# Gates and branch products of two hybrid layers with the tokens on the partitions

## The chip, the cores and the metric

The kernel runs on one core of a Trainium2 chip. The metric is the device time of one execution in microseconds (us); lower is better. The core's engines are named as in the profile: PE is TensorE (matrix products), PEld its weight loads, DVE VectorE, ACT ScalarE, POOL GpSimd, SP SyncE, which issues most transfers.

## The reference

Two blocks stand one behind the other, on 256 tokens of 1024 features in float32: a first one (pool attention, feed-forward, recurrent layer, feed-forward) and two "hybrid" layers. The change touches the hybrid layers alone. One of them, cut to what matters:

```python
h = rms_norm_2(x, g_mix)
proj = h @ w_in
... s_q, s_k, s_v, gate_logits = jnp.split(proj, offs, axis=-1)
o_mla = mla_attention(q, k, v_mla).reshape(b, s, BRANCH_WIDTH)
o_diff = (rms_norm_2(od, g_diff_out) * (1.0 - lam_init)).reshape(b, s, BRANCH_WIDTH)
o_win = window_attention(wq, wk, wv, positions, win_sink, slopes[:WIN_HEADS])
gates = jax.nn.sigmoid(gate_logits.reshape(b, s, N_BRANCH, D_MODEL))
merged = (gates[:, :, 0] * (o_mla @ w_branch[0])
          + gates[:, :, 1] * (o_diff @ w_branch[1])
          + gates[:, :, 2] * (o_win @ w_branch[2]))
x = x + merged @ w_out
```

Three gates of 1024 columns each come from the normed input (1024 features), three branch products of 1024 columns from the three attentions (512 features each). Gate times branch, summed over the three, is `merged`, which goes through the output product.

## The kernel before

**Products.** Each operand is split in a rounded part (`hi`, `xh`) and the rest (`lo`, `xl`), and `mm3` issues three matmuls for each product: hi by hi, hi by lo, lo by hi. Weights come as a stream of chunks of 1 MB through the SP queue into `st`; ACT rounds a chunk to `hi` in two halves (L262), DVE subtracts to get `lo` in two halves (L263). `st`, `hi` and `lo` have three buffers each, so the next chunk's first half on ACT waits until PE has done with the chunk three back.

**Two layouts.** The query product of a hybrid layer has tokens as the stationary operand (a slice of 128 tokens of `xh`) and 512 weight columns as the moving one; its result has tokens on the partitions. Gates and branch products are the other way round: 128 weight columns stationary, all 256 tokens moving, features on the partitions. So a gate of 1024 columns is 8 column groups by 8 slices of features by 3 = 192 matmuls of 256 columns, and a branch product is 96.

**Norm factors.** The norm's factor of each token, `r`, is applied behind the products. With features on the partitions it has to lie along the columns: `norm_rows` spreads it by two small products with `ones` (L411) into `rb`, and `times_r` (L604, DVE) multiplies a gate's bank by it before ACT takes the tanh (L1241). A sigmoid is computed as half of tanh(z/2) + 1; the half is applied when `merged` is split.

**Order around the change.** `hybrid` (phase 5 is the first hybrid layer, phase 6 the second; they stand in the names as `_5_` and `_6_`) runs the norm and some projections, and then a list of "bursts": short attention pieces (scores, transposes of the weights of a softmax, their products), and between two of them one or more steps of "filler" work from `parts()`: query, gate 0, gate 1, branch 0, gate 2, branch 1. PE keeps this program order (`InOrder`, recorded at line L207). A step is 24 matmuls of 256 columns or 12 of 512. Behind the bursts stand `branch(2)` and the output product, in four parts `kk` = 0, 2, 4, 6 of one chunk and 24 matmuls of 512 each, in banks A, A, A and O. Here the scheduler decides.

**The merge.** A branch's bank is multiplied by (gate + 1) on DVE (L1256, L1258) and summed (L1259) into `merged`, 128 by 512 four times. In `branch(2)` each quarter is split at once: ACT writes half of it to `mh` (L1263, named `xh`), DVE the rest to `ml` (L1264, named `xl`). They lie as the output product needs them, with features on the partitions.

**PSUM.** The banks are A (3), S (2), T (2) and O (1). Transposes of the softmax weights go to T; ACT copies them from there to `pT` (L853), and the O products read `pT`.

**A small input.** Behind the output product's code stands the load of `pe` (POOL queue) and its split (L311 on ACT); the scheduler places both among the bursts, where the trace shows them as `w<-in_pe_dram` and `w<-w`.

Of the kernel before, what the change touches and what calls it, by code (L numbers as in the profile page):

```python
# [11 lines left out]
F32 = mybir.dt.float32  # L12
F32R = mybir.dt.float32r
# [6 lines left out]
P = 128  # L20
S = 256
# [43 lines left out]
def _stream(a):  # L65
# [11 lines left out]
    for i in range(2):  # L77
# [11 lines left out]
        for kind, b in MERGE:  # L89
            if kind == "gate":  # L90
                out += [_kt(w, 0, KD, o[9] + b * D + j * 256, o[9] + b * D + j * 256 + 256) for j in range(4)]
                continue
# [117 lines left out]
class Net:  # L210
# [204 lines left out]
    def r_times(self, c):  # L415
        z = self.t([P, 16], "ty")
        self.nc.vector.tensor_scalar(z[:, :2], self.r, c, None, op0=ALU.mult)
        return z
# [780 lines left out]
    def hybrid(self, i, g0):  # L1199
# [5 lines left out]
        self.norm_rows()  # L1205
# [12 lines left out]
        def query():  # L1218
            b = [self.bank("A"), self.bank("A")]
            for k0 in (0, 4):  # L1220
                wh, wl = self.chunk(4, 512)
                for t in range(2):
                    for k in range(4):
                        kk, c = k0 + k, slice(t * P, t * P + P)
                        self.mm3(b[t], xh[:, kk, c], xl[:, kk, c], wh[:, k, :], wl[:, k, :], kk == 0, kk == KD - 1)
                    yield
            self.copy_out(b, 512, wq)
            self.headnorm(wq, 8, 64)

        def gate(b):  # L1230
            for jp in range(4):
                bk = self.bank("A")
                wh, wl = self.chunk(KD, 256)
                for e in range(2):
                    for k in range(KD):
                        c = slice(e * P, e * P + P)
                        self.mm3(bk[:, e * S:e * S + S], wh[:, k, c], wl[:, k, c], xh[:, k, :], xl[:, k, :], k == 0, k == KD - 1)
                    if e == 0:
                        yield
                g = self.times_r(self.t([P, 2, S], "hg"), bk).rearrange("p e s -> p (e s)")  # L1240
                nc.scalar.activation(g, g, AF.Tanh, scale=0.5)  # L1241
                gates[b].append(g)
                yield

        def branch(b):
            if b == 2:
                mh, ml = self.halves = self.t([P, KD, S], "xh", F32R), self.t([P, KD, S], "xl", F32R)
            for jp in range(4):
                if jp % 2 == 0:
                    wh, wl = self.chunk(4, 512)  # L1250
                bk = self.bank("A")
                self.fm_pair(bk, *outs[b], wh, wl, 4, (jp % 2) * 256)
                m = merged[jp // 2][:, jp % 2, :]
                g = gates[b][jp]
                if b == 0:
# [109 lines left out]
```

## Time and profile before

| | us |
|---|---|
| median of 3 runs | 1517.9 (1517.53 to 1520.76) |
| profiled execution, its own time | 1523.45 |
| its span in the trace | 1521.7 |
| mean granted TensorE clock | 0.997 |

The profiled execution is the one that the rows below show. The granted clock has two levels, 2.4 GHz (1.00 in the rows) and 1.2 GHz (0.50); a stretch that holds both shows a number between.

### The profile page before, as it was taken

To read this page: it belongs to the slowest core of one execution; us is meant where nothing else is said; L and a number is where in the kernel's file an instruction comes from. 1 tells how busy PE (TensorE), PEld (TensorE's weight loads), DVE (VectorE), ACT (ScalarE), POOL (GpSimd) and SP (SyncE) were. 2 spreads that over 40 slices of the span, in tenths; PEclk is the share of its full clock that TensorE was granted. 3 is DMA by queue.
4 is the path that set the end of the run, shared out by engine and by line. 5 is a ranking of instruction groups with operands and counts; after the bars stand their busy time and mean duration, and the time that the engine had idled before them with its cause. 6 is when DMAs were issued, how large, how long until landed. Compare 5 with 4: busy or idle time off the path is not lost.

```text
span 1521.7 us, 25363 instructions
## 1 busy us (share of the span) xinstructions
PE 1501.2 (99%) x10020; PEld 1356.4 (89%) x10020; DVE 1141.3 (75%) x2197; ACT 913.6 (60%) x1615; POOL 119.8 (8%) x109
## 2 busy tenths in 40 slices
PE   8999999999999999999999999999999999999998
PEld 6789999898999998889988999988889988999986
DVE  6659777789897777966867866668885877866666
ACT  6756555686775556755665545556856664654454
POOL 0200000000000000022530000000023250000000
PEclk9999999999999999999999999999999999999999
DMA  8445554445464554533334555544453344455551
GB/s 290 166 170 193 191 191 174 165 139 183 151 219 169 194 183 151 208 119 115 137 131 166 182 181 191 182 178 159 170 194 112 123 148 167 166 194 173 188 194 56
DMA packets 37879, 257.34 MB, mean 169 GB/s; under 512 B 4384, under 2 KB 4768, under 8 KB 8320
## 3 DMA queue, kind: packets, MB, share of 16 engines
q1 hardware_dynamic: 36576, 252.38, 46.8%
q0 software_dynamic: 896, 3.28, 0.6%
q8 instruction: 78, 1.28, 0.3%
q14 instruction: 41, 0.34, 0.1%
q10 hardware_dynamic: 288, 0.07, 0.0%
HBM read 254.66 MB, written 1.05 MB: 168 GB/s over the span
## 4 chain that ended last, share of the span: by engine, by line
PE 92%; DVE 3%; ACT 2%; POOL 1%; issue 1%; DMA 1%; SPq 0%; DVEq 0%
PE A L207 11%; PE A L279 11%; PE A L280 11%; PE A L281 10%; PE S L281 6%; PE S L280 6%; PE S L279 6%; PE T L281 6%; PE T L280 6%; PE T L279 6%; PE O L279 2%; PE O L280 2%; PE O L281 2%; PE S L207 2%; PE T L207 2%; PE O L207 1%
## 5 line engine op out<-in xcount | busy, mean ns | idle before, releaser
L263 DVE TENSOR_TENSOR lo<-st,hi 128x1024 fp32r<-128x1024 f32 (+3 forms) x480 | 573.6, 1209 | 129.4 <-ACT hi L262 126.7
L262 ACT ACTIVATE hi<-st 128x1024 fp32r<-128x1024 f32 (+3 forms) x480 | 489.2, 1043 | 264.4 <-PE T L280 109.7
L281 PE MATMUL S<-xh,lo 128*128 128x256 f32 x752 | 213.9, 284 | 0.0
L280 PE MATMUL S<-xl,hi 128*128 128x256 f32 x752 | 213.0, 283 | 0.0
L279 PE MATMUL S<-xh,hi 128*128 128x256 f32 x752 | 211.7, 282 | 0.0
L281 PE MATMUL T<-xh,lo 128*128 128x256 f32 x704 | 200.3, 285 | 0.0
L280 PE MATMUL T<-xl,hi 128*128 128x256 f32 x704 | 199.7, 284 | 0.0
L279 PE MATMUL T<-xh,hi 128*128 128x256 f32 x704 | 198.8, 282 | 0.0
L279 PEld LDWEIGHTS S<-xh,hi 128*128 128x128 f32 x752 | 142.5, 190 | 0.1
L281 PEld LDWEIGHTS S<-xh,lo 128*128 128x128 f32 x752 | 142.0, 189 | 0.1
L280 PEld LDWEIGHTS S<-xl,hi 128*128 128x128 f32 x752 | 141.5, 188 | 0.0
L279 PEld LDWEIGHTS T<-xh,hi 128*128 128x128 f32 x704 | 133.4, 189 | 1.6
L280 PEld LDWEIGHTS T<-xl,hi 128*128 128x128 f32 x704 | 132.5, 188 | 1.5
L281 PEld LDWEIGHTS T<-xh,lo 128*128 128x128 f32 x704 | 133.0, 189 | 0.1
L1074 POOL TENSOR_SCALAR s<-s,at 128x256 f32<-128x256 f32 x64 | 68.4, 1085 | 647.8 <-DVE ty L324 347.8
L280 PE MATMUL A<-lo,hg 128*128 128x512 f32 x294 | 116.3, 396 | 0.5 <-DVE lo L263 0.5
L279 PE MATMUL A<-hi,xh 128*128 128x512 f32 (+2 forms) x304 | 116.4, 385 | 0.2 <-ACT xh L389 0.2
L280 PE MATMUL A<-lo,xh 128*128 128x512 f32 (+2 forms) x304 | 116.3, 382 | 0.0
L279 PE MATMUL A<-hi,hg 128*128 128x512 f32 x294 | 116.2, 395 | 0.0
L281 PE MATMUL A<-hi,hg 128*128 128x512 f32 x294 | 116.2, 395 | 0.0
L281 PE MATMUL A<-hi,xl 128*128 128x512 f32 (+2 forms) x304 | 115.7, 383 | 0.0
L207 PE MATMUL A<-xh,hi 128*128 128x256 f32 x384 | 113.7, 296 | 0.0
(366 smaller groups left out, 3120.4 us busy)
## 6 DMA issues: line engine op xcount, KB each, us to landing
st<-in_w_dram SPq DMA_DIRECT2D x230, 1024.0 KB, 4.8
st<-in_w_dram SPq DMA_DIRECT2D x4, 832.0 KB, 4.5
st<-in_w_dram SPq DMA_DIRECT2D x2, 768.0 KB, 4.3
x<-in_x_dram SPq DMA_DIRECT2D x2, 512.0 KB, 5.0
st<-in_w_dram SPq DMA_DIRECT2D x4, 256.0 KB, 6.4
st<-in_w_dram SPq DMA_DIRECT2D x2, 512.0 KB, 3.5
w<-in_gain_dram POOLq DMA_DIRECT2D x2, 512.0 KB, 4.6
out_dram<-x SPq DMA_DIRECT2D x4, 256.0 KB, 2.0
```

The lines of the kernel that those rows point to most:

```text
L207: return lambda *a, **k: self.tc.keep_in_program_order(f(*a, **k))
L262: nc.scalar.activation(hi[:, c0:c1], st[:, c0:c1], AF.Copy)
L263: nc.vector.tensor_tensor(out=lo[:, c0:c1], in0=st[:, c0:c1], in1=hi[:, c0:c1].bitcast(F32), op=ALU.subtract)
L279: mm(out, ah, bh, start=start, stop=False)
L280: mm(out, ah, bl, start=False, stop=False)
L281: mm(out, al, bh, start=False, stop=stop)
L1074: nc.gpsimd.tensor_scalar(s[:, c], s[:, c], r[:, t:t + 1], None, op0=ALU.mult)
```

## The change

Gates and branch products now have the query's form: `columns` takes 128 tokens as the stationary operand and 512 weight columns as the moving one. A gate is 96 matmuls of 512 columns in place of 192 of 256; a branch product is 48 in place of 96. A step is 12 matmuls in place of 24, and their number stays. The chunks keep their bytes; a gate's chunk holds half the features of 512 columns in place of all the features of 256.

With tokens on the partitions `r` is a factor of each partition, so ACT takes the tanh straight from the bank with a scale of `half_r` (L1243 of the new file), and `times_r` and `norm_rows` go from the hybrid layers. `merged` has tokens on the partitions and has to be transposed for the output product: `turned(n)` does half of it by eight PE transposes (L1265) into one S and one T bank, two ACT copies (L1268) and two DVE subtractions (L1269); it is called ahead of `kk` = 0 and of `kk` = 4. New lines stand one or more further down than old ones (L279 to L281 become L280 to L282).

```diff
@@ -88,7 +88,8 @@
         out += [_kt(sq, 0, 4, 0, 512), _kt(sq, 4, 8, 0, 512)]
         for kind, b in MERGE:
             if kind == "gate":
-                out += [_kt(w, 0, KD, o[9] + b * D + j * 256, o[9] + b * D + j * 256 + 256) for j in range(4)]
+                for c in (o[9] + b * D, o[9] + b * D + 512):
+                    out += [_kt(w, 0, 4, c, c + 512), _kt(w, 4, 8, c, c + 512)]
                 continue
             wb = a["w_branch_2"][i, b]
             if b == 2:
@@ -413,8 +414,8 @@
         nc.scalar.activation(self.rb, pb[:, :S], AF.Copy)
 
     def r_times(self, c):
-        z = self.t([P, 16], "ty")
-        self.nc.vector.tensor_scalar(z[:, :2], self.r, c, None, op0=ALU.mult)
+        z = self.t([P, 2], "rg")
+        self.nc.vector.tensor_scalar(z, self.r, c, None, op0=ALU.mult)
         return z
 
 
@@ -1202,7 +1203,7 @@
         if i:
             self.layer_scalars(i)
         c, kr, skr = self.mla_prep(i, xh, xl)
-        self.norm_rows()
+        half_r = self.r_times(0.5)
         dq = self.proj(xh, xl, 8)
         dk = self.proj(xh, xl, 8)
         ch, cl = self.mla_low_rank(i, c)
@@ -1215,54 +1216,57 @@
         bursts, outs = self.heads(i, (q4, k4, v), (dq, dk, dv), (wq, wk, wv))
 
 
-        def query():
+        def columns(xh, xl, nk):
+
             b = [self.bank("A"), self.bank("A")]
-            for k0 in (0, 4):
+            for k0 in range(0, nk, 4):
                 wh, wl = self.chunk(4, 512)
                 for t in range(2):
                     for k in range(4):
                         kk, c = k0 + k, slice(t * P, t * P + P)
-                        self.mm3(b[t], xh[:, kk, c], xl[:, kk, c], wh[:, k, :], wl[:, k, :], kk == 0, kk == KD - 1)
+                        self.mm3(b[t], xh[:, kk, c], xl[:, kk, c], wh[:, k, :], wl[:, k, :], kk == 0, kk == nk - 1)
+                    yield t, (b[t] if k0 + 4 == nk else None)
+
+        def query():
+            for t, b in columns(xh, xl, KD):
+                if b is not None:
+                    nc.scalar.activation(wq[:, t, :], b, AF.Copy, scale=self.r[:, t:t + 1])
+                    if t == 1:
+                        self.headnorm(wq, 8, 64)
+                yield
+
+        def gate(b):
+            for n in range(2):
+                for t, bk in columns(xh, xl, KD):
+                    if bk is not None:
+                        g = self.t([P, 512], "hg")
+                        nc.scalar.activation(g, bk, AF.Tanh, scale=half_r[:, t:t + 1])
+                        gates[b].append(g)
                     yield
-            self.copy_out(b, 512, wq)
-            self.headnorm(wq, 8, 64)
-
-        def gate(b):
-            for jp in range(4):
-                bk = self.bank("A")
-                wh, wl = self.chunk(KD, 256)
+
+        def branch(b):
+            for n in range(2):
+                for t, bk in columns(*outs[b], 4):
+                    m, g = merged[n][:, t, :], gates[b][2 * n + t]
+                    if b == 0:
+                        nc.vector.scalar_tensor_tensor(m, g, 1.0, bk, op0=ALU.add, op1=ALU.mult)
+                    else:
+                        nc.vector.scalar_tensor_tensor(g, g, 1.0, bk, op0=ALU.add, op1=ALU.mult)
+                        nc.vector.tensor_tensor(out=m, in0=m, in1=g, op=ALU.add)
+                    yield
+
+        def turned(n, mh, ml):
+
+            for kp in range(2):
+                pt = self.bank("ST"[kp])
                 for e in range(2):
-                    for k in range(KD):
-                        c = slice(e * P, e * P + P)
-                        self.mm3(bk[:, e * S:e * S + S], wh[:, k, c], wl[:, k, c], xh[:, k, :], xl[:, k, :], k == 0, k == KD - 1)
-                    if e == 0:
-                        yield
-                g = self.times_r(self.t([P, 2, S], "hg"), bk).rearrange("p e s -> p (e s)")
-                nc.scalar.activation(g, g, AF.Tanh, scale=0.5)
-                gates[b].append(g)
-                yield
-
-        def branch(b):
-            if b == 2:
-                mh, ml = self.halves = self.t([P, KD, S], "xh", F32R), self.t([P, KD, S], "xl", F32R)
-            for jp in range(4):
-                if jp % 2 == 0:
-                    wh, wl = self.chunk(4, 512)
-                bk = self.bank("A")
-                self.fm_pair(bk, *outs[b], wh, wl, 4, (jp % 2) * 256)
-                m = merged[jp // 2][:, jp % 2, :]
-                g = gates[b][jp]
-                if b == 0:
-                    nc.vector.scalar_tensor_tensor(m, g, 1.0, bk, op0=ALU.add, op1=ALU.mult)
-                else:
-                    nc.vector.scalar_tensor_tensor(g, g, 1.0, bk, op0=ALU.add, op1=ALU.mult)
-                    nc.vector.tensor_tensor(out=m, in0=m, in1=g, op=ALU.add)
-                if b == 2:
-                    d = (slice(None), slice(2 * jp, 2 * jp + 2), slice(None))
-                    m2 = m.rearrange("p (e s) -> p e s", e=2)
-                    nc.scalar.activation(mh[d], m2, AF.Copy, scale=0.5)
-                    nc.vector.scalar_tensor_tensor(ml[d], m2, 0.5, mh[d].bitcast(F32), op0=ALU.mult, op1=ALU.subtract)
-                yield
+                    for t in range(2):
+                        c = (2 * kp + e) * P
+                        self.pe.transpose(pt[:, e * S + t * P:e * S + t * P + P], merged[n][:, t, c:c + P], self.ident)
+                d = (slice(None), slice(4 * n + 2 * kp, 4 * n + 2 * kp + 2), slice(None))
+                z = pt.rearrange("p (e s) -> p e s", e=2)
+                nc.scalar.activation(mh[d], z, AF.Copy, scale=0.5)
+                nc.vector.scalar_tensor_tensor(ml[d], z, 0.5, mh[d].bitcast(F32), op0=ALU.mult, op1=ALU.subtract)
 
         def parts():
             yield from query()
@@ -1281,9 +1285,11 @@
         self.pe = nc.tensor
         for _ in branch(2):
             pass
-        mh, ml = self.halves
+        mh, ml = self.t([P, KD, S], "xh", F32R), self.t([P, KD, S], "xl", F32R)
         acc = self.wide_banks()
         for kk in range(0, 8, 2):
+            if kk % 4 == 0:
+                turned(kk // 4, mh, ml)
             self.tm_wide(acc, mh[:, kk:kk + 2, :], ml[:, kk:kk + 2, :], kk, kk == 6)
         self.acc = acc
 
@@ -1314,8 +1320,7 @@
             for n in range(2):
                 c = slice(n * 512, n * 512 + 512)
                 nc.vector.scalar_tensor_tensor(e[t][:, c], eb[t][n], rh[:, t:t + 1], gp[:, c], op0=ALU.mult, op1=ALU.mult)
-        rg = self.t([P, 2], "rg")
-        nc.vector.tensor_scalar(rg, self.r, 0.5, None, op0=ALU.mult)
+        rg = self.r_times(0.5)
         acc = self.wide_banks()
         for kk in range(0, 8, 2):
             self.tm_wide(acc, xh[:, kk:kk + 2, :], xl[:, kk:kk + 2, :], kk, kk == 6)
```

Rows in the order of issue on an engine follow, as `out<-in` with the shape. PE at the end of `branch(2)` in the first hybrid layer, before: the names `A_5_1289` and `A_5_1290` are the last bank of `branch(2)` and the first one of the output product.

```order
L279 MATMUL A_5_1289_8682<-o_5_993_6809,hi_5_1273_8510 128x256
L280 MATMUL A_5_1289_8682<-o_5_994_6810,hi_5_1273_8510 128x256
L281 MATMUL A_5_1289_8682<-o_5_993_6809,lo_5_1274_8511 128x256
L279 MATMUL A_5_1290_8711<-hi_5_1281_8581,xh_5_1278_8577 128x512
L280 MATMUL A_5_1290_8711<-lo_5_1282_8582,xh_5_1278_8577 128x512
L281 MATMUL A_5_1290_8711<-hi_5_1281_8581,xl_5_1279_8578 128x512
```

And after, where `A_5_1282` is the last bank of `branch(2)`, `w6_5_986` and `w6_5_987` are the halves of `merged`, and `A_5_1288` is the output product's first bank:

```order
L280 MATMUL A_5_1282_8214<-hi_5_1273_8134,o_5_991_6803 128x512
L281 MATMUL A_5_1282_8214<-lo_5_1274_8135,o_5_991_6803 128x512
L282 MATMUL A_5_1282_8214<-hi_5_1273_8134,o_5_992_6804 128x512
L1265 MATMUL S_5_1292_8257<-ident_0_2_62,w6_5_986_6798 128x128 x4
L1265 MATMUL T_5_1293_8264<-ident_0_2_62,w6_5_986_6798 128x128 x4
L1265 MATMUL S_5_1300_8335<-ident_0_2_62,w6_5_987_6799 128x128
L1265 MATMUL T_5_1301_8342<-ident_0_2_62,w6_5_987_6799 128x128
L1265 MATMUL S_5_1300_8335<-ident_0_2_62,w6_5_987_6799 128x128
L280 MATMUL A_5_1288_8253<-hi_5_1279_8179,xh_5_1286_8251 128x512
L281 MATMUL A_5_1288_8253<-lo_5_1280_8180,xh_5_1286_8251 128x512
L280 MATMUL A_5_1290_8255<-hi_5_1279_8179,xh_5_1286_8251 128x512
```

Before, the output product follows `branch(2)` at once; after, eleven transposes stand between, and the first of its matmuls read `xh_5_1286`, which ACT writes. Five more (two to S, three to T) stand between `kk` = 2 and `kk` = 4.

ACT at the same place, before; `hi_5_1281`, `hi_5_1286`, `hi_5_1295` and `hi_5_1298` are the output product's chunks:

```order
L262 ACTIVATE hi_5_1281_8581<-st_5_1280_8579 128x1024 x2
L1263 ACTIVATE xh_5_1278_8577<-w6_5_988_6804 128x512
L262 ACTIVATE hi_5_1286_8647<-st_5_1285_8645 128x1024 x2
L1263 ACTIVATE xh_5_1278_8577<-w6_5_988_6804 128x512
L262 ACTIVATE hi_5_1295_8717<-st_5_1294_8715 128x1024
L1263 ACTIVATE xh_5_1278_8577<-w6_5_989_6805 128x512
L262 ACTIVATE hi_5_1295_8717<-st_5_1294_8715 128x1024
L1263 ACTIVATE xh_5_1278_8577<-w6_5_989_6805 128x512
L262 ACTIVATE hi_5_1298_8749<-st_5_1297_8747 128x1024 x2
L262 ACTIVATE hi_5_1301_8781<-st_5_1300_8779 128x1024 x2
```

And after, where the output product's chunks are `hi_5_1279`, `hi_5_1284`, `hi_5_1295` and `hi_5_1298`, and `hi_5_1303` is the first one of the feed-forward:

```order
L263 ACTIVATE hi_5_1279_8179<-st_5_1278_8177 128x1024 x2
L263 ACTIVATE hi_5_1284_8217<-st_5_1283_8215 128x1024 x2
L263 ACTIVATE hi_5_1295_8273<-st_5_1294_8271 128x1024
L1268 ACTIVATE xh_5_1286_8251<-S_5_1292_8257 128x512
L1268 ACTIVATE xh_5_1286_8251<-T_5_1293_8264 128x512
L263 ACTIVATE hi_5_1295_8273<-st_5_1294_8271 128x1024
L263 ACTIVATE hi_5_1298_8305<-st_5_1297_8303 128x1024 x2
L263 ACTIVATE hi_5_1303_8351<-st_5_1302_8349 128x1024
L1268 ACTIVATE xh_5_1286_8251<-S_5_1300_8335 128x512
L1268 ACTIVATE xh_5_1286_8251<-T_5_1301_8342 128x512
L263 ACTIVATE hi_5_1303_8351<-st_5_1302_8349 128x1024
```

The copies to `xh` stand behind the first half of `hi_5_1295` (a buffer that `branch(2)`'s last chunk holds) and, for `kk` = 4, behind the first half of `hi_5_1303` (a buffer that `kk` = 2's chunk holds). Layer 2 has the same order.

ACT around the split of `pe` (L311) in the first hybrid layer, before:

```order
L428 ACTIVATE w2_5_1203_8079<-w4_5_995_6811 128x512
L428 ACTIVATE w2_5_1204_8082<-w4_5_995_6811 128x512
L311 ACTIVATE w4_5_1307_8845<-w2_5_1306_8843 128x512
L262 ACTIVATE hi_5_1230_8213<-st_5_1229_8211 128x1024
L853 ACTIVATE pT_5_1217_8169<-T_5_1216_8164 128x512
L1241 ACTIVATE hg_5_1215_8161<-hg_5_1215_8161 128x512
L853 ACTIVATE pT_5_1219_8176<-T_5_1218_8171 128x512
L262 ACTIVATE hi_5_1230_8213<-st_5_1229_8211 128x1024
```

And after (L312):

```order
L429 ACTIVATE w2_5_1201_7799<-w4_5_993_6805 128x512
L429 ACTIVATE w2_5_1202_7802<-w4_5_993_6805 128x512
L1243 ACTIVATE hg_5_1212_7844<-A_5_1180_7703,rg_5_878_6288 128x512
L312 ACTIVATE w4_5_1309_8415<-w2_5_1308_8413 128x512
L1243 ACTIVATE hg_5_1213_7858<-A_5_1181_7704,rg_5_878_6288 128x512
L854 ACTIVATE pT_5_1215_7865<-T_5_1214_7860 128x512
L854 ACTIVATE pT_5_1217_7872<-T_5_1216_7867 128x512
L263 ACTIVATE hi_5_1229_7910<-st_5_1228_7908 128x1024 x2
```

A tanh and both copies to `pT` now follow the split at once; before, the first half of a `hi` stood ahead of both, and the tanh between them.

## Rows read from the trace of the kernel before

**Rows 1.** Page, part 1: busy time, share of span, instructions.

```profile
PE 1501.2 (99%) x10020; PEld 1356.4 (89%) x10020; DVE 1141.3 (75%) x2197; ACT 913.6 (60%) x1615; POOL 119.8 (8%) x109
```

**Rows 2.** Windows: busy us and (xcount) per engine, PEclk, DMA share, GB/s.

```profile
665.00:672.00 7.00, 6.43 (x23) 5.56 (x23) 1.59 (x4) 2.75 (x10) 1.73 (x3) 0.51 0.30 125
...
767.50:771.00 3.50, 3.50 (x19) 3.20 (x16) 3.42 (x12) 3.03 (x13) 2.95 (x2) 0.51 0.17 23
...
1135.00:1145.00 10.00, 8.86 (x68) 7.71 (x66) 5.19 (x11) 6.65 (x16) 5.98 (x5) 1.00 0.29 107
```

**Rows 3.** Timeline of PE at the first attention softmax, layer 1, then layer 2.

```profile
663.93 0.55 PE L207 MATMUL T<-ident,s 128*128 128x128 f32 x3 [1.48 <-POOL s L1074]
664.83 0.33 PE L207 MATMUL T<-ident,s 128*128 128x128 f32 x1 [0.35 <-POOL s L1074]
...
1136.37 0.55 PE L207 MATMUL T<-ident,s 128*128 128x128 f32 x3 [1.14 <-POOL s L1074]
```

**Rows 4.** Timeline of ACT, then PE, at the copy of `pe`, layer 1; PE, layer 2.

```profile
763.55 0.63 ACT L311 ACTIVATE w<-w 128x512 fp32r<-128x512 f32 x1 [7.88 <-DMA w<-in_pe_dram]
764.09 1.04 ACT L262 ACTIVATE hi<-st 128x1024 fp32r<-128x1024 f32 x1
765.03 0.58 ACT L853 ACTIVATE pT<-T 128x512 f32<-128x512 f32 x1
...
765.66 0.44 PE L207 MATMUL T<-ident,w 128*128 128x128 f32 x2 [1.80 <-ACT pT L853]
766.67 1.20 PE L207 MATMUL O<-pT,wv 128*64 128x256 f32 x8 [0.57 <-ACT pT L853]
...
1232.55 0.87 PE L207 MATMUL O<-pT,wv 128*64 128x256 f32 x6 [0.57 <-ACT pT L853]
```

**Rows 5.** Timeline of PE: first and last of the query product's 48, layer 2.

```profile
1111.28 0.40 PE L207 MATMUL A<-hi,xh 128*128 128x512 f32 x1
...
1122.20 0.40 PE L207 MATMUL A<-hi,xl 128*128 128x512 f32 x1
```

**Rows 6.** Timeline of PE: second and last of a gate run of 48, layer 2.

```profile
1143.54 0.28 PE L207 MATMUL A<-xl,hi 128*128 128x256 f32 x1
...
1149.00 0.28 PE L207 MATMUL A<-xh,lo 128*128 128x256 f32 x1
```

**Rows 7.** Timeline of PE: first and last of `branch(2)`'s 96, layer 1.

```profile
797.55 0.28 PE L279 MATMUL A<-o,hi 128*128 128x256 f32 x1
...
808.79 0.28 PE L281 MATMUL A<-o,lo 128*128 128x256 f32 x1
```

**Rows 8.** Timeline of PE around the row-norm product (L411), layer 1.

```profile
593.90 0.40 PE L281 MATMUL A<-hi,xl 128*128 128x512 f32 x1
594.30 0.49 PE L411 MATMUL T<-w,ones 128*128 128x128 f32 x2
...
595.32 0.39 PE L281 MATMUL A<-hi,xl 128*128 128x512 f32 x1
```

**Rows 9.** Timeline of PE: a norm's transposes and the first products behind them.

```profile
831.21 0.60 PE L384 MATMUL S<-ident,x 128*128 128x128 f32 x4
...
832.90 0.36 PE L279 MATMUL A<-xh,hi 128*128 128x256 f32 x1
833.10 0.28 PE L280 MATMUL A<-xl,hi 128*128 128x256 f32 x1
```

**Rows 10.** Timeline of ACT around the output product, layer 1.

```profile
809.04 1.06 ACT L262 ACTIVATE hi<-st 128x1024 fp32r<-128x1024 f32 x1 [1.89 <-PE A L280]
810.00 0.61 ACT L1263 ACTIVATE xh<-w 128x512 fp32r<-128x512 f32 x1
...
820.30 2.01 ACT L262 ACTIVATE hi<-st 128x1024 fp32r<-128x1024 f32 x2 [3.56 <-issue]
```

**Rows 11.** Timeline of PE: first low-rank product behind its transposes, layer 1.

```profile
614.97 0.44 PE L279 MATMUL A<-hi,o 128*128 128x384 f32 x1 [0.49 <-ACT o L958]
```

**Rows 12.** Groups by line, 1100 to 1300 us: busy, mean ns, idle before.

```profile
L1241 ACT ACTIVATE hg<-hg 128x512 f32<-128x512 f32 x12 | 7.4, 616 | 0.0
```

## The prediction

> **What bounds the kernel now.** I read the page first: PE is busy 99% of the span, so what PE issues and the few waits in front of it make the time; DVE (75%) and ACT (60%) matter only where PE waits for them [rows 1]. Then I went along PE's timeline through both hybrid layers for gaps. The filler keeps PE fed: between the attention pieces no gap is left but at two places a layer. At the first softmax the transposes wait for POOL, 1.48 + 0.35 us in layer 1 and 1.14 us in layer 2 [rows 3]. At the copies to `pT`, ACT has waited for the load of `pe`, with everything behind it queued; PE loses 1.80 + 0.57 us in layer 1 and 0.57 us in layer 2 [rows 4]. In layer 1 each of the two places is followed by a spell at the lower clock: the granted clock is 0.51 in 665 to 672 us and again in 767.5 to 771 us, so some 7 + 3.5 = 10.5 us at half rate, which cost about 5.2 us; around the 1.14 us wait of layer 2 it stays at 1.00 [rows 2]. The profiled execution lies 1523.45 − 1517.9 = 5.5 us above the median, about that cost. I take the two spells to be absent from most unprofiled runs, make the sum against 1523.45, and carry the difference over to the median.
>
> **The products.** At the full clock a query matmul of 512 columns takes (1122.20 − 1111.28)/47 = 232.3 ns [rows 5], a gate matmul of 256 columns (1149.00 − 1143.54)/46 = 118.7 ns [rows 6], one of `branch(2)` (808.79 − 797.55)/95 = 118.3 ns [rows 7]. Two of 256 give way to one of 512. For gates that saves 2 × 118.7 − 232.3 = 5.1 ns, for branches 4.3 ns. There are 3 gates × 96 × 2 layers = 576 such pairs and 3 × 48 × 2 = 288: 2.9 + 1.2 = **−4.1 us**. Bounds: nothing, if the new form costs as much as its columns did before, and 5 us if each pair saves as gates do and a little more. I take the rows, since the query has the very form that the gates get.
>
> The Trainium skill ("TensorE: Matmul & The Clock Gate", section "Wait — 56ns, not 53.3ns?") has a fixed part of about 2.5 ns in each matmul beside its columns. By that 864 matmuls fewer would save an estimated 2.2 us. The rows differ from it: at 2.4 GHz 512 columns are 213.3 ns and 256 are 106.7, and the rows lie 19.0 and 12.0 ns above; the sum goes by the rows.
>
> **The row norm.** `norm_rows` puts four records of L411 between products. From the L281 at 593.90 to that at 595.32 three products' time passes plus theirs: 1.42 − 3 × 0.232 = 0.72 us [rows 8]. With the same in layer 2: **−1.4 us** (0.7 to 1.5). `half_r` is one tiny DVE operation.
>
> **DVE and ACT.** 24 `times_r` leave DVE, which has no wait in front of PE in this stage; the tanh (616 ns [rows 12]) reads the bank itself. A bank is freed when ACT gets to it, but three A banks serve two at a time, so the next use of one is at least a step (12 × 232 ns = 2.8 us) off. I cost this at nothing; if ACT were late by more than a step, the excess would fall on PE. DMA and SP: the chunks have the same bytes and order, POOL's and SP's rows don't move, so nothing is late there.
>
> **The copies behind `pe`.** Before, one half of a `hi` stands between the split and the first `pT` (764.09 to 765.03 = 0.94 us), and then a tanh ahead of the second. After, it is tanh, `pT`, `pT`, `hi`: the second `pT` comes 0.94 us earlier, and the product `O<-pT` that waits for it [rows 4]. Its cover is the `hi` itself: the chunk is wanted steps later. I take −0.9 us in each layer, **−1.8 us**; bounds 0 (if the DMA lands later, or PE has moved as well) and 2.9 (all of 1.80 + 0.57 + 0.57).
>
> **The first softmax.** What PE saves before it is eaten there: its transposes wait for POOL, whose chain hangs on DVE and ACT. DVE's relief there is one `times_r`. I take 0, ± 0.6 us.
>
> **The transposes.** Sixteen transposes of a norm take 832.90 − 831.21 = 1.69 us, 106 ns each, and the first product behind them takes 200 ns in place of 118, 0.08 us [rows 9]. Two layers × 16 = 32 transposes and four switches: 3.4 + 0.35 = **+3.75 us**. That is what the tail costs if nothing waits, the lower bound.
>
> **The waits that they bring.** Now the work from `branch(2)` to the output product can no longer be split ahead. Let T1 be the end of `branch(2)` on PE. ACT's first half of the third chunk of the output product waits for the buffer that `branch(2)`'s last chunk holds, so it starts at T1 + 0.15 (before it did at 809.04, the last matmul starting at 808.79) and holds ACT for 0.96 us (809.04 to 810.00) [rows 7, 10]. In the new order the copies of the turned bank stand behind it. So the first copy runs from T1 + 1.2 to T1 + 1.8 (0.58 us, as the copy `pT` [rows 4]), though its four transposes are done at T1 + 0.5. PE fills 11 × 106 ns = 1.17 us with transposes, then waits some 0.65 us. DVE's subtraction comes behind a half of a `lo`, at about T1 + 3.2, but the order lets eight matmuls (1.9 us) run before the first that reads `xl`: no second wait. At T2, the end of `kk` = 2, it is the same with the feed-forward's first chunk, which waits for the buffer of `kk` = 2 (before: at 820.30) [rows 10]; now only five transposes (0.53 us) lie under it, and PE waits some 1.25 us. So each end costs about 1.83 us and a switch of 0.08: 3.8 us a layer, **+7.7 us**, of which 3.75 are the transposes. That a copy on the path between transposes and product stops PE is seen at the low-rank product: 0.49 us idle for ACT [rows 11]. Behind the waiting half on ACT stand only the copies and other halves that are wanted a chunk later. Upper bound: the copies of both banks behind a whole `hi`, 0.96 us more at four places, +11.5 us.
>
> **Sum.** −4.1 − 1.4 − 1.8 + 7.7 = +0.4 us, so 1523.9 us for a profiled execution with the same clock spells and **1518.3 us** for the median.
>
> **The rivals.**
> *A, faster: the copies don't wait.* If the buffer that the half `hi` waits for comes free a little before T1 and T2, or ACT takes the copies in another order than listed, PE keeps to its transposes: −7.3 + 3.75 = −3.6 us, 1514.3. For it speaks that DVE and ACT have much free time; against it the row at 809.04, where ACT's half starts right at the end of `branch(2)`. A lighter form, where T1 waits and T2 does not, gives −1.6.
> *B, slower: the new gaps bring the half clock.* In layer 1 the clock fell after 1.48 + 0.35 and after 1.80 + 0.57 us of waiting; a wait of 1.14 didn't do it [rows 2 to 4]. The gap at T2 is 1.25 us, between these, with transposes ahead of it. If it does as the longer ones did, 3.5 to 7 us at half rate cost 1.7 to 3.5 us in each layer: +0.4 + 3.5 to 7 = +4 to +7 us, 1522 to 1525. The Trainium skill ("Perfetto Trace Analysis", section "Matmul Optimizations") says that matmuls must run back to back in batches because the engine scales its power with use; it speaks against this change, which puts new gaps into a stretch that had none, and the traces bear it out in layer 1 alone.
> *C, the cheaper matmuls are not cheaper.* The gain of −4.1 is absent or halved: +2.5 to +4.5, 1520.4 to 1522.4. Against it speaks the query, with the same operands and the same form.
> *D, the `pT` copies gain nothing* because the load of `pe` lands relative to PE as before and the stall was made by it: +2.2, 1520.1.
>
> **How the numbers follow.** The forecast holds 0.42, D 0.10, A with its lighter form 0.24, B 0.16, C 0.08. A measurement of this kernel can tell about 0.2% (3 us) from no change: A's full form is beyond it (0.2), B and most of C beyond it on the other side (0.24), the rest inside (0.56). The likeliest case alone runs from 1516 to 1521. For 8 in 10 the range takes in A's full form and the lower half of B: 1513.8 to 1523.0.
>
> **What would show it.** In the changed profile: gate and branch matmuls of 512 columns every 232 to 234 ns; no L411 in the hybrid layers; PE idle before the first product of `kk` = 0 of about 0.65 us and before `kk` = 4 of about 1.25 us, both ended by ACT's L1268, with ACT's L263 just ahead of it; the wait for `pT` shorter by 0.9 us; the clock at 1.00 behind the output product's start. The prediction is wrong if the two waits are under 0.3 us each (then A), if a stretch at 0.5 follows one of them (B), or if the A banks make PE wait for the tanh, which I cost at nothing.

## The result, and the profile after

The changed kernel takes 1527.85 us (median of 4, 1527.04 to 1528.78), the kernel before beside it 1519.33: a ratio of 1.0057 (95% interval 1.0039 to 1.0074). It is slower by 8.5 us, above the range that was given. The profiled execution has a span of 1527.0 us against 1521.7. A later set of runs gave 1524.28 against 1517.72, 1.0035 (1.0021 to 1.0049). The kernel before has medians from 1517.72 to 1519.33 in the sets of runs below, but its lowest time lies between 1516.16 and 1516.59 us in the four later sets.

The page's first part; PE has 840 matmuls fewer in the trace than in [rows 1] and is busy for as long:

```profile
PE 1500.6 (98%) x9180; PEld 1312.3 (86%) x9180; DVE 1123.5 (74%) x2175; ACT 912.7 (60%) x1609; POOL 122.6 (8%) x109
```

A run of 24 gate matmuls of the second hybrid layer on PE's timeline, second and last:

```profile
1143.85 0.39 PE L208 MATMUL A<-lo,xh 128*128 128x512 f32 x1
...
1148.97 0.39 PE L208 MATMUL A<-hi,xl 128*128 128x512 f32 x1
```

(1148.97 − 1143.85)/22 = 232.7 ns each, as forecast; two of [rows 6] take 237.4.

The turning, on PE's timeline, at `kk` = 0 and `kk` = 4 of the first hybrid layer, and ACT's rows beside it:

```profile
804.91 0.60 PE L1265 MATMUL S<-ident,w 128*128 128x128 f32 x4
...
806.58 0.33 PE L1265 MATMUL S<-ident,w 128*128 128x128 f32 x1 [0.41 <-DVE w L1255]
806.71 0.50 PE L280 MATMUL A<-hi,xh 128*128 128x512 f32 x1
...
817.98 0.38 PE L1265 MATMUL S<-ident,w 128*128 128x128 f32 x2
...
819.77 0.50 PE L280 MATMUL A<-hi,xh 128*128 128x512 f32 x1 [1.08 <-ACT xh L1268]
```

```profile
805.11 1.06 ACT L263 ACTIVATE hi<-st 128x1024 fp32r<-128x1024 f32 x1 [3.59 <-PE A L282]
806.08 0.58 ACT L1268 ACTIVATE xh<-S 128x512 fp32r<-128x512 f32 x1
...
818.17 1.06 ACT L263 ACTIVATE hi<-st 128x1024 fp32r<-128x1024 f32 x1 [3.56 <-PE O L282]
819.14 0.58 ACT L1268 ACTIVATE xh<-S 128x512 fp32r<-128x512 f32 x1
```

At each place ACT's half of a `hi` stands ahead of the first copy, and the product starts behind the copy: from 804.9 to 806.71 and from 817.98 to 819.77, 1.8 us each. This is the order of events that was forecast. The two other places where PE waits are not as forecast. ACT around the split of `pe`, and PE there, first layer, then the second:

```profile
761.20 0.63 ACT L312 ACTIVATE w<-w 128x512 fp32r<-128x512 f32 x1 [7.04 <-DMA w<-in_pe_dram]
761.74 0.67 ACT L1243 ACTIVATE hg<-A,rg 128x512 f32<-128x512 f32 x1
762.31 1.07 ACT L854 ACTIVATE pT<-T 128x512 f32<-128x512 f32 x2
763.26 1.06 ACT L263 ACTIVATE hi<-st 128x1024 fp32r<-128x1024 f32 x1
...
766.03 0.51 ACT L916 ACTIVATE s<-s,at 128x256 f32<-128x256 f32 x1 [0.75 <-DVE at L912]
...
768.38 0.45 ACT L1162 ACTIVATE qk<-T,vp 128x256 f32<-128x256 f32 x1
...
1230.78 0.63 ACT L312 ACTIVATE w<-w 128x512 fp32r<-128x512 f32 x1 [7.22 <-DMA w<-in_pe_dram]
```

```profile
762.95 0.44 PE L208 MATMUL T<-ident,w 128*128 128x128 f32 x2 [1.80 <-ACT pT L854]
763.44 0.87 PE L208 MATMUL O<-pT,wv 128*64 128x256 f32 x6
...
768.98 0.41 PE L208 MATMUL T<-ident,s 128*128 128x128 f32 x2 [1.05 <-ACT qk L1162]
...
1232.53 0.44 PE L208 MATMUL T<-ident,w 128*128 128x128 f32 x2 [1.98 <-ACT pT L854]
```

The two copies to `pT` do follow the tanh, and the wait of 0.57 us in [rows 4] is gone; but PE waits as long as before for the first copy (1.80 us), then 1.05 us at the next transposes for `qk`, which had no wait before; and in layer 2 it waits 1.98 us where it had waited 0.57 in all. By the views of waits PE stands 4.8 us there in place of 2.9, after and then before:

```profile
PE T L208 <- ACT pT L854: 3.8, 2, 2.0
...
PE T L208 <- ACT qk L1162: 1.0, 1, 1.0
```

```profile
PE T L207 <- ACT pT L853: 1.8, 1, 1.8
PE O L207 <- ACT pT L853: 1.1, 2, 0.6
```

Where the wait for `qk` comes from is seen on DVE, after, and on DVE and ACT, before, first layer:

```profile
764.36 1.23 DVE L264 TENSOR_TENSOR lo<-st,hi 128x1024 fp32r<-128x1024 f32 x1 [1.81 <-ACT hi L263]
765.51 0.48 DVE L912 CUSTOM_DVE_ANT_0 s<-S,bias,negsink 128x256 f32<-128x256 f32 x1
```

```profile
765.16 1.22 DVE L263 TENSOR_TENSOR lo<-st,hi 128x1024 fp32r<-128x1024 f32 x1 [3.75 <-ACT hi L262]
...
766.90 0.48 DVE L911 CUSTOM_DVE_ANT_0 s<-S,bias,negsink 128x256 f32<-128x256 f32 x1
...
767.46 0.50 ACT L915 ACTIVATE s<-s,at 128x256 f32<-128x256 f32 x1
...
769.80 0.46 ACT L1161 ACTIVATE qk<-T,vp 128x256 f32<-128x256 f32 x1
```

DVE's part of the softmax stands behind the `lo` of the `hi` that was moved back. Counted from the start of the split (763.55 before, 761.20 after), `lo` starts at 3.16 us in place of 1.61, DVE's softmax row at 4.31 in place of 3.35, ACT's, which waits 0.75 us for it, at 4.83 in place of 3.91, and `qk` at 7.18 in place of 6.25.

In layer 2 the split itself came later against PE. Before, it started 2.1 us ahead of the transposes:

```profile
1229.43 0.63 ACT L311 ACTIVATE w<-w 128x512 fp32r<-128x512 f32 x1 [6.08 <-DMA w<-in_pe_dram]
...
1231.54 0.44 PE L207 MATMUL T<-ident,w 128*128 128x128 f32 x2
```

After, it started at 1230.78, 0.2 us behind the moment at which PE came to them (1232.53 − 1.98 = 1230.55).

The first softmax, in layer 1 and then layer 2:

```profile
663.27 0.33 PE L208 MATMUL T<-ident,s 128*128 128x128 f32 x1 [1.74 <-POOL s L1075]
664.17 0.90 PE L208 MATMUL T<-ident,s 128*128 128x128 f32 x3 [0.57 <-POOL s L1075]
...
1135.73 0.33 PE L208 MATMUL T<-ident,s 128*128 128x128 f32 x1 [1.02 <-POOL s L1075]
1136.64 0.55 PE L208 MATMUL T<-ident,s 128*128 128x128 f32 x3 [0.57 <-POOL s L1075]
```

In layer 1 it is 1.74 + 0.57 = 2.31 us; before, it was 2.40, for a third wait stands behind the two that [rows 3] show:

```profile
665.73 0.90 PE L207 MATMUL T<-ident,s 128*128 128x128 f32 x3 [0.57 <-POOL s L1074]
```

In layer 2 it is 1.02 + 0.57 us against 1.14. The windows (columns as in [rows 2]) show the clock:

```profile
663.90:670.60 6.70, 6.43 (x17) 5.24 (x18) 1.62 (x4) 2.64 (x9) 1.43 (x3) 0.50 0.32 136
805.00:820.00 15.00, 13.50 (x66) 10.87 (x65) 7.94 (x9) 6.82 (x9) 0.00 (x0) 1.00 0.53 196
1134.00:1138.00 4.00, 2.41 (x15) 1.79 (x14) 0.97 (x1) 1.77 (x3) 2.58 (x2) 1.00 0.50 160
1233.90:1237.20 3.30, 3.30 (x9) 2.49 (x8) 3.26 (x10) 2.55 (x9) 1.05 (x1) 0.50 0.01 2
1275.00:1291.00 16.00, 14.50 (x70) 11.64 (x69) 9.05 (x11) 7.93 (x10) 0.00 (x0) 1.00 0.50 185
```

Half clock behind the first softmax and behind the second layer's wait for `pT`, 6.7 + 3.3 us; full clock through both turnings. The kernel before had some 10 us at half clock too [rows 2], so in the two profiled executions the clock makes little difference.

### The profile page after: what moved, and what is told of

The parts are those of the page before. It is cut to its first block, busy times and chain, and to the rows that moved or that the text cites. A ratio compares the mean times of both kernels' runs of the same rounds, so it can differ in the third digit from the quotient of the medians.

```text
span 1527.0 us, 23642 instructions
## 1 busy us (share of the span) xinstructions
PE 1500.6 (98%) x9180; PEld 1312.3 (86%) x9180; DVE 1123.5 (74%) x2175; ACT 912.7 (60%) x1609; POOL 122.6 (8%) x109
## 3 DMA queue, kind: packets, MB, share of 16 engines
HBM read 254.66 MB, written 1.05 MB: 167 GB/s over the span
## 4 chain that ended last, share of the span: by engine, by line
PE 91%; DVE 3%; POOL 2%; ACT 2%; issue 1%; DMA 1%; SPq 0%; DVEq 0%
PE A L208 11%; PE A L280 11%; PE A L281 11%; PE A L282 10%; PE S L282 6%; PE S L281 6%; PE S L280 6%; PE T L282 6%; PE T L281 6%; PE T L280 6%; PE O L280 2%; PE O L281 2%; PE O L282 2%; PE S L208 2%; PE T L208 2%; POOL s L1075 1%
## 5 line engine op out<-in xcount | busy, mean ns | idle before, releaser
L282 PE MATMUL S<-xh,lo 128*128 128x256 f32 x752 | 214.1, 285 | 0.0
L281 PE MATMUL S<-xl,hi 128*128 128x256 f32 x752 | 213.2, 283 | 0.0
L280 PE MATMUL S<-xh,hi 128*128 128x256 f32 x752 | 211.8, 282 | 0.0
L282 PE MATMUL T<-xh,lo 128*128 128x256 f32 x704 | 200.5, 285 | 0.0
L281 PE MATMUL T<-xl,hi 128*128 128x256 f32 x704 | 199.8, 284 | 0.0
L280 PE MATMUL T<-xh,hi 128*128 128x256 f32 x704 | 198.9, 283 | 0.0
L280 PEld LDWEIGHTS S<-xh,hi 128*128 128x128 f32 x752 | 142.6, 190 | 0.1
L282 PEld LDWEIGHTS S<-xh,lo 128*128 128x128 f32 x752 | 142.1, 189 | 0.1
L281 PEld LDWEIGHTS S<-xl,hi 128*128 128x128 f32 x752 | 141.6, 188 | 0.0
L280 PEld LDWEIGHTS T<-xh,hi 128*128 128x128 f32 x704 | 133.5, 190 | 1.6
L281 PEld LDWEIGHTS T<-xl,hi 128*128 128x128 f32 x704 | 132.6, 188 | 1.5
L282 PEld LDWEIGHTS T<-xh,lo 128*128 128x128 f32 x704 | 133.0, 189 | 0.1
L1075 POOL TENSOR_SCALAR s<-s,at 128x256 f32<-128x256 f32 x64 | 69.1, 1096 | 647.8 <-DVE ty L327 348.4
L280 PE MATMUL A<-hi,xh 128*128 128x512 f32 (+2 forms) x304 | 116.6, 386 | 2.4 <-ACT xh L1268 2.2
L281 PE MATMUL A<-lo,hg 128*128 128x512 f32 x294 | 116.4, 396 | 0.5 <-DVE lo L264 0.5
L280 PE MATMUL A<-hi,hg 128*128 128x512 f32 x294 | 116.2, 395 | 0.0
L282 PE MATMUL A<-hi,hg 128*128 128x512 f32 x294 | 116.2, 395 | 0.0
L281 PE MATMUL A<-lo,xh 128*128 128x512 f32 (+2 forms) x304 | 115.6, 380 | 0.0
L282 PE MATMUL A<-hi,xl 128*128 128x512 f32 (+2 forms) x304 | 113.9, 381 | 0.0
L208 PE MATMUL A<-hi,xh 128*128 128x512 f32 x224 | 93.8, 419 | 0.0
```

The source lines that it names most:

```text
L208: return lambda *a, **k: self.tc.keep_in_program_order(f(*a, **k))
L280: mm(out, ah, bh, start=start, stop=False)
L281: mm(out, ah, bl, start=False, stop=False)
L282: mm(out, al, bh, start=False, stop=stop)
L1075: nc.gpsimd.tensor_scalar(s[:, c], s[:, c], r[:, t:t + 1], None, op0=ALU.mult)
```

## The experiments

Each was timed in up to five rounds beside the kernel before; medians and ratios to it follow. What lies between kernels of different sets is read from medians, good to 1 or 2 us, and beside them from the lowest times, which come at a granted clock of 0.999 or 1.000.

**1 and 2. The load of `pe` on SP's queue**, in the changed kernel and in the one before:

```diff
-        nc.gpsimd.dma_start(pe, self.ap["pe"][i])
+        nc.sync.dma_start(pe, self.ap["pe"][i])
```

> The changed kernel with one line moved: the load of `pe` is issued on SP's queue in place of POOL's; by the order ACT's split then stands behind the two copies to `pT`. Theory 1 (the load, late behind POOL's backlog, holds ACT and through it PE for 2.0 us in each layer, and a spell at half clock follows): the waits for `pT` go, 2 x 2 us and 1.7 to 3.4 us of clock, 1521 us (1519.5 to 1523). Rival (the wait only moves to the next thing that POOL gives late, or the load delays the chunk behind it on SP): 1526 to 1529.

> The kernel before with the same one line moved. Theory 1: the waits of 1.80 + 0.57 us and 0.57 us go and the spell behind the first of them, 1515.5 to 1517. It then lies 2 to 4 us below the changed kernel with the same line (the forecast's sum without its term for `pe`: -4.1 - 1.4 + 7.7 = +2.2). Rival (the difference of 8.5 us has nothing to do with `pe`): both fall alike and stay 7 to 9 us apart.

Changed: 1521.39 us, 1.0009 (0.9998 to 1.0019). Before: 1515.90, 0.9980 (0.9970 to 0.9991). Both lose every wait for `pT`. The kernel before gains 3.2 us, the changed one 6.5 or 2.9, by which of its two sets one takes. The medians stay 5.5 us apart, more than the 2 to 4 expected. The lowest times are 1518.45 and 1515.45, 3.0 apart, which is within it; but ten of the twelve times of the changed kernel lie more than 1.8 us above its lowest, at granted clocks from 0.999 down to 0.996, and five of twelve of the other, at 0.998 and 0.997. So the rest of the 5.5 us comes and goes between executions of one program.

**3. The turning earlier**, each half where PE has other work to do behind it:

```diff
-        for _ in branch(2):
-            pass
         mh, ml = ...
+        for j, _ in enumerate(branch(2)):
+            if j == 2:
+                turned(0, mh, ml)
...
-            if kk % 4 == 0:
-                turned(kk // 4, mh, ml)
+            if kk == 2:
+                turned(1, mh, ml)
```

> The changed kernel with the first turning one bank of branch(2) earlier and the second ahead of kk = 2 in place of kk = 4. Theory 1 (the two waits of 0.65 and 1.25 us in each layer are ACT's copies that stand on the path, and cost only themselves): -3.8 us, 1524 us (1523 to 1525). Rival (the gaps also bring the half clock, or their cost is given back): -6 to -9 us, 1519 to 1522, or no change.

1520.38 us, 1.0004 (0.9993 to 1.0015): 7.5 below the first set of the changed kernel, 3.9 below the second. The median lies where the rival put it, not in the 1523 to 1525 of the theory. The profile shows why the first number misleads: the waits for `pT` and `qk` are 0.8 + 2.1 us here and 3.8 + 1.0 in the changed kernel's profile, though ACT's and POOL's orders there are the same. Against the second set it is the 3.8 us of the theory.

**4. No turning** (the transposes are left out, `merged` is read as it lies):

> The changed kernel without the transposes: the output product reads merged as it lies, split on ACT and DVE during branch(2) as before the change, so that the turning of merged is left out. Theory 1: the whole term of the turning goes, 7.4 us, 1520.5 us (1519.5 to 1521.5); products and row norm keep their gain of some 5 us, so the rest above the kernel before, some 1 us and the 5 us of gain, is the wait for `pe` and what follows it. Rival (the turning costs more than its waits and transposes, through the clock): 1516 to 1518.

1516.56 us, 0.9979 (0.9969 to 0.9990), in the rival's range and lower than the theory's, again with a shorter wait for `pT` (1.3 us in all, and 2.1 for `qk`). The second set of the changed kernel lies 7.7 us above it, the term of the turning; no half clock is in its profile.

**5. The changed kernel again**, since the same order gave long and short waits. In the first profile POOL's and DVE's timelines are

```profile
749.83 4.09 POOL L898 TENSOR_SCALAR bias<-distw 128x512 f32<-128x512 f32 x2
754.02 4.34 POOL L1075 TENSOR_SCALAR s<-s,at 128x256 f32<-128x256 f32 x4
758.31 0.59 POOL L1297 DMA_DIRECT2D w<-in_pe_dram  x1
```

```profile
749.77 2.77 DVE L264 TENSOR_TENSOR lo<-st,hi 128x1024 fp32r<-128x1024 f32 x2 [0.59 <-ACT hi L263]
```

> The changed kernel itself, beside the others. In its profile POOL's L898 started 0.06 us behind DVE's first half of a `lo` and took 2.52 us in place of 1.49, which put the load of `pe` and ACT's split off; in the run with the load on SP the two started 0.03 us apart, POOL kept its 1.49 us and DVE was the slower one. Theory 1 (a race between the two engines, decided by hundredths of a us, with the wait for `pT` hanging on it): the times fall into two groups, one at 1520 to 1523 us with short waits, one at 1526 to 1529 with waits of 2 us. Rival (the wait follows from the order alone): all at 1526 to 1529.

1524.28 us (1522.08 to 1526.23), and in its profile POOL's and DVE's timelines are

```profile
749.07 3.07 POOL L898 TENSOR_SCALAR bias<-distw 128x512 f32<-128x512 f32 x2
752.23 3.63 POOL L1075 TENSOR_SCALAR s<-s,at 128x256 f32<-128x256 f32 x4
755.81 0.58 POOL L1297 DMA_DIRECT2D w<-in_pe_dram  x1
```

```profile
749.03 3.31 DVE L264 TENSOR_TENSOR lo<-st,hi 128x1024 fp32r<-128x1024 f32 x2 [0.59 <-ACT hi L263]
```

The program is the same. In the first profile DVE's `lo` leads POOL's L898 by 0.06 us and POOL's pair takes 4.09 us; in the second it leads by 0.04 us, POOL keeps 3.07 and DVE's pair takes 3.31 in place of 2.77. With the four L1075 behind (4.34 us in place of 3.63) that makes 758.31 or 755.81 for the load, 2.5 us, of which 0.76 is the pair's earlier start. The other layers and profiles with the load on POOL show the same two outcomes: in both layers of the first profile POOL's pair takes 4.1 us (DVE ahead by 0.06 and 0.05 us), in both layers of experiments 3, 4 and 5 it takes 3.1 (0.03 or 0.04). So the load's issue hangs on which of the two engines is held up, a race by these rows; what decides it they do not show.

The wait hangs on more than that. From the load's issue to ACT's split pass 2.89 us in the first profile and 3.72 in the second, layer 1; in the kernel before it is 4.70 us in layer 1 (758.85 to 763.55) and 2.91 in layer 2 (1226.52 to 1229.43), and there PE waits 1.80 us for the first copy in layer 1 and not at all in layer 2.

The times do not fall into two groups (1522.1 to 1526.2), and the profiled execution, with its early load, is the longest of the six; so the expectation holds for the race and not for the times. The granted clock goes from 1.000 at the two lowest times to 0.997 at the three highest. In this profile a half clock came behind the softmax of layer 2, which it had not in the first:

```profile
1136.10:1139.30 3.20, 3.20 (x9) 2.51 (x8) 1.46 (x3) 1.30 (x5) 0.15 (x1) 0.50 0.41 174
```

**6, 7 and 8. Pairs.** The early turning with the load on SP; no turning with the load on SP; and the first of these with one filler step more ahead of the first transposes:

```diff
-            (4,), (1, f(mq, 0)), (2, f(ms, 0), f(mq, 1)),
+            (4,), (1, f(mq, 0)), (3, f(ms, 0), f(mq, 1)),
```

> The changed kernel with both the early turning and the load of `pe` on SP. Theory 1: the load on SP alone gave 1521.4; the waits of the turning are 0.55 + 1.15 us in each layer, so -3.4 to -3.8: 1517.8 us (1516.5 to 1519). Rival (the early turning gained 7.5 by itself because the gaps cost more than their length): 1513 to 1515.

> The changed kernel without the transposes (the turning of merged is left out) and with the load of `pe` on SP; against the kernel before with the load on SP it holds the products and the row norm alone. Theory 1: 3.9 us for 864 fewer matmuls and 1.2 for the row norm below 1515.5 at the full clock, 1510.5 us in the fastest runs, median 1510.5 to 1513. Rival (the products give 2.2 us, by the fixed part of 2.5 ns alone): 1512.1 in the fastest runs.

> As the early turning with the load on SP, and one filler step more between the first scores and the first transposes of softmax weights (3 in place of 2; the last burst has one fewer). Theory: the wait of PE for POOL there, 1.7 + 0.4 us in the first and about 1.9 us in the second hybrid layer, is covered by a step of 2.8 us, and the half clock behind it does not come: -4 us and less spread, 1512 to 1514 us. Rival (POOL is late by as much at the next softmax): no change, 1517 to 1518.

1515.94 (0.9982, 0.9972 to 0.9991), 1512.95 (0.9964, 0.9951 to 0.9977) and 1510.04 us (0.9944, 0.9928 to 0.9960). The sixth lies 5.5 us below experiment 1 where 3.4 to 3.8 were expected; the tenth below and the eighth, which have no wait for POOL, are 4.5 apart. The seventh decides nothing: its lowest time, 1512.2, equals the rival's number, but the wait for POOL and its half clock were still in it. The eighth lost them; it is lower than the 1512 to 1514 expected, and its runs lie within 1.4 us (1509.92 to 1511.31). In its view of waits PE has none left for POOL's `s`, `pT`, `qk` or the turning's `xh`. It beats both kernels, by 7.7 us the one before.

**9, 10 and 11. Without the other stalls**: the load on SP and the filler step in the kernel before, in the changed one, and in the changed one without the turning.

> The kernel before with the load of `pe` on SP and the third filler step ahead of the first transposes. Theory: the waits of 3.5 us for POOL and the spells at half clock go too, 1511.5 to 1513 us, with little spread. It is the clean base for the next two.

> The changed kernel with the same two edits. Theory 1 (without the other stalls the change is worth the sum of its direct terms): -3.9 for the products, -1.2 for the row norm, +7.4 for the turning: 2 to 3 us above the kernel before with the same edits, 1514 to 1515, and 3.5 to 4 above the early turning with both (1510.0). Rival (the gaps of the turning bring spells at half clock, or the difference of 5 us and more between the two kernels stays): 5 to 8 us above, with more spread.

> The changed kernel with the same two edits and without the transposes (the turning of merged is left out). Theory 1: 5.1 us below the kernel before with the two edits (3.9 for 864 fewer matmuls, 1.2 for the row norm), some 1507 us. Rival (2.5 ns for each matmul saved, 2.2 us, and 1.2): 3.4 us below, 1508.7.

1515.21 (0.9980), 1514.55 (0.9976) and 1506.26 us (0.9924). The ninth was expected at 1511.5 to 1513, and the tenth 2 to 3 us above it; as run, the tenth lies 0.7 us below. The tenth less the eleventh is the turning, 8.3 us; PE's timelines of the two put it at 3.83 us in layer 1 and 3.84 in layer 2 (from the last matmul of `branch(2)` to the last of the output product, 26.12 less 22.29 and 26.13 less 22.29). Its waits, in both layers:

```profile
PE A L280 <- ACT xh L1268: 2.2, 2, 1.1
PE S L1265 <- DVE w L1255: 0.8, 2, 0.4
```

The ninth was no clean base. Its view of waits has two that no other kernel has, 2.9 us: branch 1 came one step earlier and waited for its input. The tenth has the same step and no such wait.

```profile
PE A L207 <- ACT o L1038: 1.7, 2, 0.9
PE A L207 <- DVE o L1039: 1.2, 2, 0.7
```

**12. The clean base**: as the ninth, with one step fewer at another burst.

```diff
-            (1, f(mt, 3), f(ds, 0, 0)), (2, f(wkt), f(mo, 3)),
+            (1, f(mt, 3), f(ds, 0, 0)), (1, f(wkt), f(mo, 3)),
```

> The kernel before with the load of `pe` on SP, the third filler step ahead of the first transposes, and one step fewer at the last first-attention output, so that branch 1 starts no earlier than it did. In the profile of the last base branch 1 waited 0.88 + 0.71 us in a layer for its input (2.9 us in both layers), since it had moved one step forward. Theory 1: those 2.9 us go, 1512.3 us (1511.7 to 1513), and the changed kernel with the two edits (1514.55) stands 2.2 us above it, the sum of the direct terms. Rival (the change is even, as the last pair said): 1514 to 1515.5.

1511.18 us (1510.98 to 1511.80), 0.9953 (0.9939 to 0.9968), and its view of waits has none for POOL's `s`, `pT`, `qk` or branch 1's `o`. It lies 4.0 us below the ninth, 1.1 more than the waits that went, and a little below the 1511.7 to 1513 expected.

So without the other stalls the change costs 1514.55 − 1511.18 = 3.4 us: 8.3 for the turning less 1511.18 − 1506.26 = 4.9 for products and row norm. The lowest times (1513.46, 1510.98, 1506.05) give 2.5, 7.4 and 4.9. The two kernels of this pair differ in that one step as well; with the step the same (ninth and tenth) they are even.

## Why the prediction was wrong, point by point

- **Products and row norm: right.** −4.1 and −1.4 were forecast, −4.9 measured (experiments 12 and 11). From the rows after, 576 × (237.4 − 232.7) = 2.7 us come from the gates; that leaves about 1 us each for branches and row norm. By the 2.5 ns a matmul of the Trainium skill ("TensorE: Matmul & The Clock Gate", section "Wait — 56ns, not 53.3ns?") it would have been an estimated 2.2 + 1.4 = 3.6; the measurement decides for the rows, in which a gate's pair gave way with a gain of 4.7 ns.
- **The turning: right**, mechanism, place and size. +7.7 forecast, 7.7 by the timelines, 8.3 by the medians. One detail: at `kk` = 0 one transpose also waits 0.41 us for DVE's last sum (L1255), inside the time that ACT takes anyway.
- **The copies behind `pe`: this step failed.** "I take −0.9 us in each layer" rested on the sentence that the cover is the `hi` itself, "wanted steps later". The copies came as forecast: the product `O<-pT` starts 2.24 us behind the split (763.44 − 761.20) in place of 3.12 (766.67 − 763.55). But the `hi` has a second reader: DVE's `lo`, and DVE's softmax rows stand behind that `lo`. They slipped by 0.96 us, ACT's softmax waited for them, `qk` came 0.93 us later behind the split, and PE, which was 0.9 us earlier, stood 1.05 us at the next transposes. With the load on POOL this wait of 1.03 to 1.05 us is in seven of eight places (both layers of the first profile and of experiments 3 to 5); the eighth is layer 2 of the first profile, where PE ran at half clock.
- **"POOL's and SP's rows don't move, so nothing is late there": this failed with it.** PE reaches the transposes earlier than before, and the load's issue stands behind a chain of POOL instructions that took 1.7 us longer in the first profile (from 749.83 to 758.31, against 752.10 to 758.85 before). This is rival D, with a price on top. By the lowest times the load's stall is worth 1.1 us before (1516.54 − 1515.45) and 3.6 after (1522.08 − 1518.45): +2.5 us in place of −1.8. By the medians it is 3.2 before (experiment 2) and 2.9 or 6.5 after (experiment 1), so −0.3 or +3.3.
- **The first softmax: right in the wait, not in the clock.** I took 0 ± 0.6; by the views of waits it went from 3.5 to 3.9 us. Without it the lowest time falls by 5.0 us in the changed kernel (1518.45 − 1513.46) and by 4.5 in the one before (1515.45 − 1510.98): +0.5. The medians fall by 6.8 (experiments 1 and 10) and 4.7 (2 and 12): +2.1. The rest goes with the half clock. It came behind this wait in layer 2 in the profiles of experiments 1, 3, 5 and 7, but not in those of the changed kernel's first run, 4 and 6, which have the same wait, and in neither of the two profiles of the kernel before that have it. Four of seven and none of two are too few to say that the change brings it.
- **The carrying over to the median: a second step that failed.** The prediction took the spells at half clock to be absent from most unprofiled runs and subtracted 5.5 us. All four runs of the changed kernel have a granted clock of 0.996 to 0.998, and their median lies only 0.9 us below the profiled execution (1528.78). In the second set two of six runs are at 1.000, and the median lies 2.0 us below it. The runs of the kernel before range from 1516.5 to 1524.2 us at a granted clock from 1.000 to 0.996, and its profiled execution was near the upper end.
- **Sum.** The measured median lies 9.6 us above the forecast one, 4.9 of it in the terms and 4.6 in the carrying over. In the profiled executions the terms make +5.3 us (1523.45 to 1528.78) where +0.4 was forecast: +7.7 for the turning, −4.9 for products and row norm, +1.9 for `pT` and `qk` in place of −1.8, +0.4 at the softmax, and +0.5 for the first loads of the program, for which PE waits 6.3 us in place of 5.8. That adds up to 5.6.
- **Rival B named a loss that was there, at another place.** The clock stayed at 1.00 through both turnings; the half clock followed the old waits. The Trainium skill's sentence that matmuls should run back to back in batches ("Perfetto Trace Analysis", section "Matmul Optimizations") fits those, not the turning's gaps of up to 1.1 us.
- **Two readings in the prediction.** [rows 3] leave out a third wait of 0.57 us in layer 1. The lighter form of rival A, by the prediction's own waits, is −3.6 + 2 × 0.65 = −2.3, not −1.6; neither changes the forecast.

What stays open: why POOL's pair is held in one execution and not in another, at recorded leads of 0.03 to 0.06 us, was not forced either way by an experiment; nor was the time that the load takes to land (2.9 to 4.7 us); and which execution gets a half clock behind a wait of 1 to 2 us.

## What to carry to other kernels

Before an instruction that is moved out of the way is costed at nothing, list everything that reads its result and everything that is queued behind those readers on their engines, and ask which of these PE reaches next: here a rounding on ACT, moved back by 1.5 us, held up a softmax on DVE, and the wait that shrank at one place came back at the following one. And look first at the waits that stand in a kernel already: the load on POOL's queue, ahead of a copy that PE needs, cost 1 to 6.5 us here, where the rewriting of the products and the row norm brought 4.9; and one line on another queue, one filler step and an earlier call for the transposes turned a loss of 6.6 to 8.5 us into a gain of 7.7. Of that gain the rewriting itself, with the waits of its turning hidden, holds about 1 us (1511.18 against 1510.04 us), no more than sets of runs differ by.

## What the runs showed of the hardware

Two engines that run at once can hold each other up. POOL's pair of L898 took 3.07 us when POOL kept its pace and 4.09 when DVE's `lo` led it by 0.06 us; with a lead of 0.04 us it was DVE's pair that took 3.31 us in place of 2.77. One and the same program showed both. The Trainium skill ("SBUF — State Buffer", section "SBUF: two separate sides") says that VectorE and GpSimd share one pair of ports as an exclusive lock, and that whichever instruction starts first keeps it while the other blocks. The first profile agrees, in both layers; in the second DVE was ahead by the record and POOL kept its pace all the same, so at such a distance the recorded starts don't tell the winner.

The half clock came behind waits of 1.02 + 0.57 us in one execution (layer 2 of experiment 5, granted clock 0.50) and not in another of the same program (layer 2 of the first profile, 1.00).
